# One change in five places of a two-layer diffusion kernel: half groups of first weights, other PSUM banks and earlier silus, split weights kept for a last pass run backwards

## The chip, the cores and the metric

One NeuronCore of one Trainium2 chip runs the whole program. The metric is the time of one execution in device microseconds (us). The core has five engines that work side by side and wait for each other by semaphores: TensorE (PE in the profile, and PEld for its weight loads), VectorE (DVE), ScalarE (ACT), GpSimd (POOL) and SyncE (SP, which only issues DMAs here). Each engine takes its instructions strictly in the order in which the program was built.

## The reference

Two post-norm layers over 256 latent tokens and 256 context tokens of width 2048, in float32.

```python
for l in range(DEPTH):                       # DEPTH = 2
    shift_l, scale_l, gate_l = split(silu(c) @ mod_w[l] + mod_b[l], 3)      # the same from c_ctx for the context
    hl = xl * (1.0 + scale_l) + shift_l;  hc = xc * (1.0 + scale_c) + shift_c
    if l % 2 == 0:   # one input projection, 2048 -> 6400: pooling mixer | RWKV-7 in both directions
        yl, yc = (concat([multiscale_pool(a), rwkv], -1) * silu(gate)) @ w_out
    else:            # one input projection: attention of 16 heads with 4 key heads, rotary, RMSNorm of q and k
        yl = (attention(q, k, v) * silu(g)) @ w_out
    xl = layer_norm(ALPHA * xl + gate_l * yl)   # and xc likewise after layer 0; the output is xl
```

## The kernel before

Each large product is made three times from split operands: a weight or an activation is cast to fp32r by ScalarE (`whi`, `hh`), the rest `x - hi` is taken by VectorE or GpSimd (`wlo`, `hl`), and `mm3` runs hi·hi, hi·lo and lo·hi, each a matmul of 512 columns ("wide" below), into one PSUM bank. All weights come from HBM for each use. There are eight banks under the tags `acc`, `tr` and `prep` (two each), `cx` and `cz` (one each).

The order of TensorE's instructions is fixed by hand when the program is built: the parts of the kernel are generators that a small loop (`merge`) steps in turn by priority and by a reckoned clock `self.t`; a `yield` of a number says after how many reckoned us a generator wants to go on, a `yield` of a process that it waits for that process's end. The orders of the other engines are set by the tile framework, which places instructions by a timeline of its own, and earlier if they are marked `high_priority`. The helper `run_fill` takes a list of units (a source in HBM and a function that makes the matmuls), loads `rawbufs - 1` units ahead and splits one unit ahead.

The stages, in order:

- `begin`. Eight groups `g`. The modulation weights (`modA`, eight loads of 512 KB for a group: four for the shift, four for the scale) meet the conditioning vector in narrow matmuls (`prep<-wrow,sc`); the row that results is copied, turned into columns (`prep<-comb,wrow`) and applied to two 128-row tiles of x (`modulate`, which appends the split tiles to `self.h`). Then the first six chunks of the input projection use these two tiles, three chunks for each of two `wF` loads (384 KB): `first(g, 0)` and `first(g, 1)`, 18 wide matmuls each. The units stand in the order: the eight modulation units of group g+1, then `first(g, 0)`, `first(g, 1)`. The buffers for raw weights are eight of 1024 columns.
- The middle. `rwkv` with its helpers (`lora` first) is a long chain of small matmuls; `fill0`, at a lower priority, fills TensorE with the other 44 chunks of the input projection, and `gemvs` computes the modulation of layer 1 and the gates from `modB`. Each chunk ends in `spill`, which for the 16 gate chunks applies `silu` (L315 to L319: two ScalarE steps, a VectorE step between them, a third ScalarE step, and a VectorE product that reads the bank for the last time).
- `out0`, the output projection of layer 0 in passes of 512 output columns: pass 0 over the banks acc, acc, tr, tr, pass 1 over prep, prep, cx, cz, pass 2 over the first set again, then columns 3 in two halves. Its activations `y[k]` are made by `gated_acts` and `gate_acts`: 16 products, each cast by ScalarE (L78, `hh`) and subtracted by VectorE or GpSimd (L74, `hl`) in turn. Their pool takes the place of the pool of `self.h`, so they start when the last input chunk is done.
- `norm0`, twice: LayerNorm of two token tiles, transposes to `prep`, then the modulation of layer 1 as (x·A + B) from PSUM on VectorE (`hraw`, L989), a cast and a subtraction. GpSimd meanwhile applies the LayerNorm's weights to the other copy (L1004, L1005: 32 steps).
- `layer1`: keys, values, queries, gates, attention heads, filled like the middle.
- `out1`, the output projection of layer 1: passes over columns 0, 1, 2 for both token tiles, then columns 3 for tile 0 and for tile 1, each with all 16 weights loaded and split anew. `final(t)` normalises: two steps each on ScalarE and VectorE, the weight `lg` on VectorE, the bias `lb` on VectorE or GpSimd, and four stores.

## Time and profile before

| what | value |
|---|---|
| time, median of 3 runs | 1881.06 us (1879.25 to 1887.59) |
| the profiled execution: its time, its span | 1879.39 us, 1877.6 us |
| TensorE busy | 1711.6 us, 91% of the span |
| VectorE, ScalarE, GpSimd busy | 1048.8, 728.6, 660.8 us |
| granted clock, mean over the span | 0.964 |

Time minus span is 1.8 us, which the trace doesn't show. TensorE is the engine with the least idle time; "PEclk" is the share of full speed that its clock was granted, where 1.00 is 2.4 GHz and 0.50 is 1.2 GHz.

### The profile page before, as it was taken

What the parts mean: (1) busy time and instruction counts of PE and PEld (TensorE: products, weight loads), DVE (VectorE), ACT (ScalarE), POOL (GpSimd) and SP (SyncE); (2) the same over time, 40 slices, a digit from 0 to 9 for tenths busy, and PEclk for the clock granted to TensorE, in tenths of its full rate; (3) what the DMA queues carried; (4) which work ended last, traced back from release to release, by engine and by line L of the source; (5) the groups of instructions that cost most, each with busy time, mean ns of one, the idle gap of its engine ahead of it and who ended that gap; (6) DMA issues with size and microseconds to landing.
All of it is one profiled execution on the core that took longest, in us unless ns stands there. A gap on an engine that the chain in (4) does not pass through costs nothing. (4 is left out here: it accounts for less than half of the span.)

```text
span 1877.6 us, 38910 instructions
## 1 busy us (share of the span) xinstructions
PE 1711.6 (91%) x15584; PEld 1286.9 (69%) x15584; DVE 1048.8 (56%) x1992; ACT 728.6 (39%) x1402; POOL 660.8 (35%) x565
## 2 busy tenths in 40 slices
PE   6888989999999999999997899699988999999995
PEld 3656666666676666677675577588766878888773
DVE  2224467666676758384845522411495487666458
ACT  1115634242425242434332243322453455555444
POOL 1114233323232324142413344544655442231234
PEclk9889999999999989899989999899999999999998
DMA  9886844544544445454456454444653543443754
GB/s 377 298 316 198 301 157 152 164 148 147 157 155 157 164 129 166 126 175 157 138 164 197 145 183 138 127 127 129 205 152 128 160 150 112 127 135 96 258 192 166
DMA packets 162213, 322.72 MB, mean 172 GB/s; under 512 B 17648, under 2 KB 28400, under 8 KB 160880
## 3 DMA queue, kind: packets, MB, share of 16 engines
q1 hardware_dynamic: 153680, 299.15, 49.0%
q10 hardware_dynamic: 8352, 21.09, 3.5%
q8 instruction: 122, 2.00, 0.4%
q14 instruction: 59, 0.48, 0.1%
HBM read 290.25 MB, written 29.92 MB: 171 GB/s over the span
## 5 line engine op out<-in xcount | busy, mean ns | idle before, releaser
L74 POOL TENSOR_TENSOR wlo<-wrow,whi 128x512 fp32r<-128x512 f32 (+1 forms) x347 | 474.6, 1370 | 948.8 <-ACT whi L206 842.6
L206 ACT CAST whi<-wrow 128x512 fp32r<-128x512 f32 (+1 forms) x528 | 328.3, 625 | 609.3 <-PE acc L87 189.2
L87 PE MATMUL acc<-hh,whi 128*128 128x512 f32 (+1 forms) x992 | 385.9, 389 | 11.7 <-ACT whi L206 9.0
L87 PE MATMUL acc<-hh,wlo 128*128 128x512 f32 (+1 forms) x992 | 384.8, 388 | 7.3 <-POOL wlo L74 3.6
L87 PE MATMUL acc<-hl,whi 128*128 128x512 f32 (+1 forms) x992 | 383.4, 387 | 0.0
L87 PEld LDWEIGHTS acc<-hh,whi 128*128 128x128 f32 x992 | 190.5, 192 | 56.1 <-ACT whi L206 13.0
L87 PEld LDWEIGHTS acc<-hh,wlo 128*128 128x128 f32 x992 | 190.7, 192 | 51.8 <-issue 9.0
L87 PEld LDWEIGHTS acc<-hl,whi 128*128 128x128 f32 x992 | 190.5, 192 | 43.7 <-issue 12.4
L74 DVE TENSOR_TENSOR wlo<-wrow,whi 128x512 fp32r<-128x512 f32 (+1 forms) x181 | 144.1, 802 | 134.6 <-ACT whi L206 134.2
L87 PE MATMUL tr<-wlo,hh 128*128 128x512 f32 x224 | 91.0, 406 | 6.6 <-DVE wlo L74 3.4
L87 PE MATMUL tr<-whi,hl 128*128 128x512 f32 x224 | 90.5, 404 | 0.0
L87 PE MATMUL tr<-whi,hh 128*128 128x512 f32 x224 | 89.8, 401 | 0.0
L87 PE MATMUL prep<-gw,sc 128*32 128x128 f32 x2048 | 79.4, 287 | 8.8 <-issue 5.2
L87 PEld LDWEIGHTS prep<-gw,sc 128*32 128x32 f32 x2048 | 53.4, 113 | 17.6 <-issue 7.8
L87 PE MATMUL acc<-whi,hh 128*128 128x512 f32 x128 | 52.1, 407 | 13.4 <-DVE ev L319 11.8
L87 PEld LDWEIGHTS tr<-wlo,hh 128*128 128x128 f32 x224 | 42.5, 190 | 18.3 <-DVE wlo L74 5.1
L87 PE MATMUL acc<-wlo,hh 128*128 128x512 f32 x128 | 52.1, 407 | 3.0 <-POOL wlo L74 3.0
L87 PE MATMUL prep<-wrow,sc 128*32 128x256 f32 x512 | 39.0, 444 | 17.3 <-DMA wrow<-in_modA 17.2
L461 POOL TENSOR_TENSOR BK<-T,D 64x512 f32<-64x512 f32 x32 | 46.4, 1451 | 23.2 <-PE cz L87 11.8
L87 PE MATMUL acc<-whi,hl 128*128 128x512 f32 x128 | 51.9, 406 | 0.5 <-DVE hl L74 0.5
L87 PEld LDWEIGHTS tr<-whi,hh 128*128 128x128 f32 x224 | 42.5, 190 | 10.6 <-issue 0.5
L87 PEld LDWEIGHTS tr<-whi,hl 128*128 128x128 f32 x224 | 42.5, 190 | 9.9 <-issue 0.7
(373 smaller groups left out, 3096.4 us busy)
## 6 DMA issues: line engine op xcount, KB each, us to landing
gw<-in_modB SPq DMA_DIRECT2D x256, 256.0 KB
wrow<-in_wA SPq DMA_DIRECT2D x176, 256.0 KB
wrow<-in_modA SPq DMA_DIRECT2D x64, 512.0 KB
wrow<-in_w SPq DMA_DIRECT2D x112, 256.0 KB
wrow<-in_woA SPq DMA_DIRECT2D x80, 256.0 KB
wrow<-in_wo SPq DMA_DIRECT2D x80, 256.0 KB
wrow<-in_w1g SPq DMA_DIRECT2D x64, 256.0 KB
pd<-ev SPq DMA_DIRECT2D x50, 256.0 KB
```

What stands on the lines that cost most here:

```text
L74: e.tensor_tensor(out=out, in0=raw, in1=hi.bitcast(F32), op=ALU.subtract)
L87: self.nc.tensor.matmul(out, a, b, start=start, stop=stop)
L206: self.lastsplit = self.nc.scalar.copy(hi, raw)
L461: nc.gpsimd.tensor_tensor(out=BK[hs, :, 1 - h, :], in0=c8(k)[hs], in1=c8(ew)[hs], op=ALU.mult)
```

## The change

Five places change together.

1. `begin`: the units stand in half groups: four modulation units of group g+1, `first(g, 0)`, the other four, `first(g, 1)`. Since `first(g, 0)` now comes nearer to the modulation that it needs, it waits (in the planning) until `self.h` holds its tiles. `gemvs` plans its first step 20 us after the start of the middle instead of 10.
2. `spill`: the gates' silus are marked `high_priority`. `out0`: the two sets of banks are swapped, so that pass 0 uses prep, prep, cx and cz and waits, in the planning, for the end of `rwkv` and `gemvs`, which used these banks. The banks of keys and values in `layer1` are swapped to match.
3. `norm0`: every second pair of tiles gets its A and B on ScalarE instead of VectorE, and the planned step between pairs is 1.6 us instead of 1.0.
4. `out1`: in the fourth pass (columns 3, tile 0) the last six split weights are kept; the fifth (tile 1) runs over the 16 weights backwards and takes those six without loading or splitting them. From the third pass on there are 7 buffers for raw and 9 for split weights (before: 8 and 5).
5. `final`: z·lg is computed ahead on GpSimd, slice by slice; then three of four slices take two VectorE steps (b = lg·r1 + lb, z = z·r0 + b), and the first takes two ScalarE and two GpSimd steps.

```diff
--- before.py
+++ after.py
@@ -182,14 +182,17 @@
 
     def run_fill(self, units):
 
         units = list(units)
         raws, splits = [], []
         for i, (_, f, *_) in enumerate(units):
             while len(raws) < min(len(units), i + self.rawbufs - 1):
-                raws.append(self.load(units[len(raws)][0]))
+                src = units[len(raws)][0]
+                raws.append(src if isinstance(src, int) else self.load(src))
             while len(splits) < min(len(units), i + 2):
-                splits.append(raws[len(splits)] if len(units[len(splits)]) > 2 else self.split(raws[len(splits)]))
-            yield from f(splits[i])
+                raw = raws[len(splits)]
+                splits.append(raw if isinstance(raw, int) or len(units[len(splits)]) > 2 else self.split(raw))
+            yield from f(self.kept[splits[i]] if isinstance(splits[i], int) else splits[i])
             raws[i] = splits[i] = None
 
     def row(self):
@@ -278,6 +281,8 @@
 
             def first(g, half):
                 def f(w):
+                    while len(self.h) < 2 * g + 2:
+                        yield 0.3
                     for i in range(3):
                         for j in range(2):
                             k = 2 * g + j
@@ -288,9 +293,8 @@
             mods = [self.mod_cols(0, 2 * g, 256, "prep") + self.mod_cols(1, 2 * g, 256, "prep", lambda g=g: modulate(g)) for g in range(8)]
             units = list(mods[0])
             for g in range(8):
-                if g < 7:
-                    units += mods[g + 1]
-                units += [first(g, 0), first(g, 1)]
+                m = mods[g + 1] if g < 7 else []
+                units += m[:4] + [first(g, 0)] + m[4:] + [first(g, 1)]
             self.merge(self.spawn(self.run_fill(units), 9))
             self.wset(wp, 512, 4, 3)
         for m, a in zip(self.FIRST, acc):
@@ -301,7 +305,8 @@
         if m < M_G:
             self.nc.scalar.copy(ev, ps)
         else:
-            self.silu(ev, ps)
+            with self.tc.high_priority():
+                self.silu(ev, ps)
         self.nc.sync.dma_start(self.pd[m], ev)
         self.there.add(m)
 
@@ -808,7 +813,7 @@
         biases(0)
         for _ in range(3):
             ahead()
-        yield 10.0
+        yield 20.0
         bank, ends = self.pt("prep"), []
         for r in range(256):
             i, k = divmod(r, KT)
@@ -846,14 +851,17 @@
 
     GPACE = 7.0
 
-    def outproj(self, w, y, ks, passes, done):
-        acc = {}
+    def outproj(self, w, y, ks, passes, done, keep=0):
+        acc, self.kept = {}, {}
 
         def unit(j, i, k):
             n, toks, tags = passes[j]
 
             def g(wt):
+                if keep and j == len(passes) - 2 and i >= KT - keep:
+                    self.kept[k] = wt
                 if i == 0:
                     acc[j] = [self.pt(t, bufs=1 if t in ("cx", "cz") else None) for t in tags]
                 if j == 0 and callable(y[k]):
@@ -862,9 +870,12 @@
                     yield from self.mm3(a, wt, y[k], i == 0, i == KT - 1, slice(0, 512), slice(t * 128, t * 128 + 128), flip=True)
                 if i == KT - 1:
                     yield from done(n, toks, acc.pop(j))
+            if keep and j == len(passes) - 1 and i < keep:
+                return k, g
             return w[n, k // 2][:, k % 2 * 512:k % 2 * 512 + 512], g
 
-        return self.run_fill([unit(j, i, k) for j in range(len(passes)) for i, k in enumerate(ks)])
+        ks = list(ks)
+        return self.run_fill([unit(j, i, k) for j in range(len(passes)) for i, k in enumerate(ks[::-1] if keep and j == len(passes) - 1 else ks)])
 
     def gated_acts(self, main):
 
@@ -956,8 +967,10 @@
                 return self.y[k] or ys[k]
 
         yield self.joined
+        yield main
+        yield self.gemv_p
         self.norms, self.h1at = [], {}
-        a, b = ("acc", "acc", "tr", "tr"), ("prep", "prep", "cx", "cz")
+        b, a = ("acc", "acc", "tr", "tr"), ("prep", "prep", "cx", "cz")
         passes = [(0, range(4), a), (1, range(4), b), (2, range(4), a), (3, (0, 1), b[:2]), (3, (2, 3), b[2:])]
         yield from self.outproj(io["woA"], Y(), self.korder, passes, done)
 
@@ -986,13 +999,16 @@
                     self.tp(tp[:, k - k0, t * 128:t * 128 + 128], z[2 * s + t][:, k * 128:k * 128 + 128], self.cst["ident"])
             raw = lp.tile([128, 2, 256], F32, tag="hraw", name="hraw", bufs=2)
             for k in (k0, k0 + 1):
-                nc.vector.tensor_scalar(raw[:, k - k0, :], tp[:, k - k0, :], self.A[:, k, s:s + 1], self.B[:, k, s:s + 1], op0=ALU.mult, op1=ALU.add)
+                if k0 % 4:
+                    nc.scalar.activation(raw[:, k - k0, :], tp[:, k - k0, :], AF.Identity, scale=self.A[:, k, s:s + 1], bias=self.B[:, k, s:s + 1])
+                else:
+                    nc.vector.tensor_scalar(raw[:, k - k0, :], tp[:, k - k0, :], self.A[:, k, s:s + 1], self.B[:, k, s:s + 1], op0=ALU.mult, op1=ALU.add)
                 hh, hl = self.h1[k]
                 w = slice(s * 256, s * 256 + 256)
                 nc.scalar.copy(hh[:, w], raw[:, k - k0, :])
                 self.sub(hl[:, w], raw[:, k - k0, :], hh[:, w], "v")
                 self.h1at[s, k] = self.t + 3.0
-            yield 1.0
+            yield 1.6
         if s:
 
             lg = self.bcast(lp, io["lng"][0:1, :], "gb0")
@@ -1063,9 +1079,9 @@
         self.kpost = []
         lat, ctx4 = (2, 3), range(4)
 
-        units = self.proj(4, (0, 1), ("tr", "tr"), self.keys)
-        units += self.proj(5, ctx4, ("acc", "acc", "cx", "cz"), self.values)
-        units += self.proj(4, lat, ("tr", "tr"), self.keys)
+        units = self.proj(4, (0, 1), ("cx", "cz"), self.keys)
+        units += self.proj(5, ctx4, ("acc", "acc", "tr", "tr"), self.values)
+        units += self.proj(4, lat, ("cx", "cz"), self.keys)
         yield from self.run_fill(units)
         for p in self.norms:
             yield p
@@ -1251,21 +1267,33 @@
                 nc.vector.tensor_tensor(out=tmp, in0=a, in1=gb[:, w], op=ALU.mult)
                 nc.vector.scalar_tensor_tensor(out=z[t][:, w], in0=z[t][:, w], scalar=ALPHA, in1=tmp, op0=ALU.mult, op1=ALU.add)
                 self.bn(lp, z[t], t, n)
+                if n == 2:
+                    yield loads
+                    for i in range(3):
+                        v = slice(i * 512, i * 512 + 512)
+                        nc.gpsimd.tensor_tensor(out=z[t][:, v], in0=z[t][:, v], in1=lg[:, v], op=ALU.mult)
                 if n == 3:
-                    yield loads
+                    nc.gpsimd.tensor_tensor(out=z[t][:, w], in0=z[t][:, w], in1=lg[:, w], op=ALU.mult)
                     final(t)
             if n == 1:
                 self.l1p.__exit__(None, None, None)
-                self.wset(self.ctx.enter_context(self.tc.tile_pool(name="wlast", bufs=1)), 512, 8, 5)
+                self.wset(self.ctx.enter_context(self.tc.tile_pool(name="wlast", bufs=1)), 512, 7, 9)
             yield 0.0
 
         def final(t):
             rs = self.norm(lp, t)
             for n in range(4):
                 w = slice(n * 512, n * 512 + 512)
-                self.apply(rs, z[t][:, w], n % 2)
-                nc.vector.tensor_tensor(out=z[t][:, w], in0=z[t][:, w], in1=lg[:, w], op=ALU.mult)
-                (nc.vector if n % 2 else nc.gpsimd).tensor_tensor(out=z[t][:, w], in0=z[t][:, w], in1=lb[:, w], op=ALU.add)
+                b = lp.tile([128, 512], F32, tag="fb", name="fb", bufs=2)
+                if n:
+                    nc.vector.scalar_tensor_tensor(out=b, in0=lg[:, w], scalar=rs[:, 1:2], in1=lb[:, w], op0=ALU.mult, op1=ALU.add)
+                    nc.vector.scalar_tensor_tensor(out=z[t][:, w], in0=z[t][:, w], scalar=rs[:, 0:1], in1=b, op0=ALU.mult, op1=ALU.add)
+                else:
+                    nc.scalar.activation(b, lg[:, w], AF.Identity, scale=rs[:, 1:2])
+                    nc.scalar.activation(z[t][:, w], z[t][:, w], AF.Identity, scale=rs[:, 0:1])
+                    nc.gpsimd.tensor_tensor(out=b, in0=b, in1=lb[:, w], op=ALU.add)
+                    nc.gpsimd.tensor_tensor(out=z[t][:, w], in0=z[t][:, w], in1=b, op=ALU.add)
                 nc.sync.dma_start(io["out"][t * 128:(t + 1) * 128, w], z[t][:, w])
 
         class Y(list):
@@ -1273,7 +1301,7 @@
                 return self.y1[k] or (lambda: self.until(k))
 
         passes = [(0, (0, 1), ("acc", "acc")), (1, (0, 1), ("tr", "tr")), (2, (0, 1), ("acc", "acc")), (3, (0,), ("tr",)), (3, (1,), ("tr",))]
-        yield from self.outproj(io["wo1"], Y(), range(KT), passes, done)
+        yield from self.outproj(io["wo1"], Y(), range(KT), passes, done, 6)
 
     def until(self, k):
         while self.y1[k] is None:
```

The order of the loads that SyncE issues at the beginning, `modA` being modulation weights, `wA` weights of the middle that are loaded ahead, and `wF` the first chunks' weights. Before:

```order
L146 DMA par<-in_par 128x340
L200 DMA wrow<-in_modA 128x1024 x9
L200 DMA wrow<-in_wA 128x512 x4
L200 DMA wrow<-in_modA 128x1024 x6
L200 DMA wrow<-in_wA 128x512 x3
L200 DMA wrow<-in_modA 128x1024
L200 DMA wrow<-in_wF 128x768 x2
L200 DMA wrow<-in_modA 128x1024 x8
L200 DMA wrow<-in_wF 128x768 x2
```

Now:

```order
L146 DMA par<-in_par 128x340
L203 DMA wrow<-in_modA 128x1024 x9
L203 DMA wrow<-in_wA 128x512 x4
L203 DMA wrow<-in_modA 128x1024 x3
L203 DMA wrow<-in_wF 128x768
L203 DMA wrow<-in_modA 128x1024 x2
L203 DMA wrow<-in_wA 128x512 x3
L203 DMA wrow<-in_modA 128x1024 x2
L203 DMA wrow<-in_wF 128x768
L203 DMA wrow<-in_modA 128x1024 x4
L203 DMA wrow<-in_wF 128x768
```

The first `wF` now stands behind 12 loads of `modA` and 4 of `wA` instead of 16 and 7, and from there on one `wF` follows each four `modA`, where two followed each eight.

GpSimd's order where the input projection ends and pass 0 of `out0` begins (`hl` are the halves of y, `wlo` those of weights; the first row ends with the weights of units 0 and 1 of pass 0). Before:

```order
L74 TENSOR_TENSOR wlo<-wrow,whi 128x512 x36
L74 TENSOR_TENSOR hl<-AR_12222,hh 128x512
L74 TENSOR_TENSOR hl<-AR_12269,hh 128x512
L74 TENSOR_TENSOR hl<-GR_12330,hh 128x512
L74 TENSOR_TENSOR hl<-GR_12385,hh 128x512
L74 TENSOR_TENSOR hl<-AR_12432,hh 128x512
L74 TENSOR_TENSOR hl<-AR_12487,hh 128x512
L74 TENSOR_TENSOR hl<-GR_12574,hh 128x512
L74 TENSOR_TENSOR wlo<-wrow,whi 128x512
L74 TENSOR_TENSOR hl<-GR_12743,hh 128x512
L74 TENSOR_TENSOR wlo<-wrow,whi 128x512 x74
```

Now:

```order
L74 TENSOR_TENSOR wlo<-wrow,whi 128x512 x36
L74 TENSOR_TENSOR hl<-AR_12225,hh 128x512
L74 TENSOR_TENSOR hl<-AR_12286,hh 128x512
L74 TENSOR_TENSOR hl<-GR_12333,hh 128x512
L74 TENSOR_TENSOR hl<-GR_12388,hh 128x512
L74 TENSOR_TENSOR hl<-AR_12435,hh 128x512
L74 TENSOR_TENSOR hl<-AR_12490,hh 128x512
L74 TENSOR_TENSOR hl<-GR_12572,hh 128x512
L74 TENSOR_TENSOR wlo<-wrow,whi 128x512 x4
L74 TENSOR_TENSOR hl<-GR_12741,hh 128x512
L74 TENSOR_TENSOR wlo<-wrow,whi 128x512 x71
```

The weights of unit 2 still stand behind seven `hl`; what moved is that four weights instead of one come before the last `hl`. On ScalarE, too, the last gate's second and third silu step (L317 and L318, now L322 and L323) stay behind 14 casts of `hh`.

VectorE's order at the end (`z_18370` is token tile 0, `z_18371` tile 1; `tmp<-tr` is the first reading of the last pass's bank). Before:

```order
L778 TENSOR_SCALAR z_18370<-z_18370,rs 128x512 x2
L74 TENSOR_TENSOR wlo<-wrow,whi 128x512
L1267 TENSOR_TENSOR z_18370<-z_18370,lg 128x512 x4
L1268 TENSOR_TENSOR z_18370<-z_18370,lb 128x512
L1251 TENSOR_TENSOR tmp<-tr,gb 128x512
L1268 TENSOR_TENSOR z_18370<-z_18370,lb 128x512
L1252 SCALAR_TENSOR_TENSOR z_18371<-z_18371,tmp 128x512
L763 BN_STATS bns<-z_18371 128x6
```

Now:

```order
L1290 SCALAR_TENSOR_TENSOR fb<-lg,rs,lb 128x512
L1291 SCALAR_TENSOR_TENSOR z_18370<-z_18370,rs,fb 128x512
L1290 SCALAR_TENSOR_TENSOR fb<-lg,rs,lb 128x512
L1291 SCALAR_TENSOR_TENSOR z_18370<-z_18370,rs,fb 128x512
L1290 SCALAR_TENSOR_TENSOR fb<-lg,rs,lb 128x512
L1267 TENSOR_TENSOR tmp<-tr,gb 128x512
L1291 SCALAR_TENSOR_TENSOR z_18370<-z_18370,rs,fb 128x512
L1268 SCALAR_TENSOR_TENSOR z_18371<-z_18371,tmp 128x512
L768 BN_STATS bns<-z_18371 128x6
```

No weight is split any more among the last steps of tile 0, but one step of tile 0 still stands between the two readings for tile 1.

Of TensorE's order three counts matter. Between the input chunks' start and the first matmul of `lora` there were 65 wide matmuls and a step of `gemvs`, and now 70 and none. Between two groups of four transposes in the second `norm0` there were 5 wide matmuls, and now 7. On GpSimd's side of the same stretch, the 32 steps on z have 4 splits of weights among them before and 5 now.

## Rows read from the trace of the kernel before

**Rows 1.** The page: span, busy times, the group of weight splits on GpSimd.

```profile
span 1877.6 us, 38910 instructions
...
PE 1711.6 (91%) x15584; PEld 1286.9 (69%) x15584; DVE 1048.8 (56%) x1992; ACT 728.6 (39%) x1402; POOL 660.8 (35%) x565
...
L74 POOL TENSOR_TENSOR wlo<-wrow,whi 128x512 fp32r<-128x512 f32 (+1 forms) x347 | 474.6, 1370 | 948.8 <-ACT whi L206 842.6
```

**Rows 2.** Windows in `begin` (length; PE, PEld, DVE, ACT, POOL busy; clock, DMA, GB/s).

```profile
28.00:45.20 17.20, 13.43 (x69) 9.51 (x66) 7.51 (x16) 4.14 (x6) 2.55 (x2) 1.00 1.03 403
45.20:49.40 4.20, 4.20 (x53) 2.70 (x55) 0.27 (x1) 0.00 (x0) 0.00 (x0) 1.00 0.52 180
49.40:63.10 13.70, 11.52 (x61) 8.69 (x54) 4.58 (x11) 2.91 (x4) 1.81 (x1) 0.75 1.00 350
```

**Rows 3.** The same view, by stages of the program.

```profile
35.70:158.00 122.30, 109.80 (x729) 80.47 (x730) 36.72 (x74) 24.13 (x34) 15.55 (x10) 0.92 0.78 282
158.00:184.60 26.60, 20.28 (x94) 14.93 (x93) 14.24 (x12) 17.56 (x27) 16.66 (x18) 0.87 0.92 277
...
1393.80:1429.70 35.90, 26.71 (x119) 20.00 (x118) 35.33 (x54) 14.26 (x34) 35.39 (x39) 0.95 0.27 81
1829.50:1858.10 28.60, 24.85 (x97) 17.05 (x96) 28.12 (x40) 19.11 (x32) 14.21 (x9) 1.00 0.62 202
```

**Rows 4.** DMA issues: count and KB each.

```profile
wrow<-in_modA SPq DMA_DIRECT2D x64, 512.0 KB
...
wrow<-in_wF SPq DMA_DIRECT2D x16, 384.0 KB
xt<-in_xT ACTq DMA_DIRECT2D x16, 256.0 KB
```

**Rows 5.** TensorE's timeline in `begin` (start, us; idle before, releaser).

```profile
35.73 0.79 PE L87 MATMUL acc<-hh,whi 128*128 128x512 f32 x1 [0.77 <-ACT whi L206]
...
65.80 3.66 PE L87 MATMUL prep<-wrow,sc 128*32 128x256 f32 x64
...
77.57 0.40 PE L87 MATMUL tr<-hh,whi 128*128 128x512 f32 x1
...
80.37 0.39 PE L87 MATMUL cx<-hh,whi 128*128 128x512 f32 x1
```

**Rows 6.** Timeline where pass 0 of `out0` starts.

```profile
1173.98 2.17 ACT L78 CAST hh<-AR 128x512 fp32r<-128x512 f32 x4
...
1175.19 3.44 POOL L74 TENSOR_TENSOR hl<-AR,hh 128x512 fp32r<-128x512 f32 x2 [0.26 <-ACT hh L78]
...
1184.12 3.42 DVE L74 TENSOR_TENSOR hl<-GR,hh 128x512 fp32r<-128x512 f32 x2
1185.29 1.71 POOL L74 TENSOR_TENSOR hl<-GR,hh 128x512 fp32r<-128x512 f32 x1
1187.46 0.67 DVE L319 TENSOR_TENSOR ev<-ev,acc 128x512 f32<-128x512 f32 x1
...
1188.19 0.79 PE L87 MATMUL acc<-whi,hh 128*128 128x512 f32 x1 [11.83 <-DVE ev L319]
...
1193.17 1.57 POOL L74 TENSOR_TENSOR wlo<-wrow,whi 128x512 fp32r<-128x512 f32 x1 [6.18 <-ACT whi L206]
```

**Rows 7.** Timeline in the second `norm0`.

```profile
1406.20 0.98 DVE L989 TENSOR_SCALAR hraw<-prep,mA,mB 128x256 f32<-128x256 f32 x2
...
1407.33 0.63 PE L101 MATMUL prep<-cc,z 128*128 128x128 f32 x4 [1.63 <-DVE hraw L989]
...
1414.14 0.51 PE L87 MATMUL tr<-wlo,hh 128*128 128x512 f32 x1 [3.06 <-POOL wlo L74]
```

**Rows 8.** Timeline of the end.

```profile
1857.67 0.40 PE L87 MATMUL tr<-whi,y1l 128*128 128x512 f32 x1
...
1863.67 0.69 DVE L763 BATCH_NORM_STATS2 bns<-z 128x6 f32<-128x512 f32 x1
...
1868.60 4.67 POOL L1268 TENSOR_TENSOR z<-z,lb 128x512 f32<-128x512 f32 x2 [5.51 <-DVE z L1267]
```

## The prediction

> **What bounds the kernel now.** I read the page first: TensorE is busy for 1711.6 of 1877.6 us, and no other engine comes near [rows 1]. The time can fall only where TensorE stands idle (166 us in all) or where its clock is below full; work on other engines counts only as a wait of TensorE. So I took TensorE's idle times in order of time, put windows around the stretches that the change touches, and read the timeline there. Five places matter.
>
> `begin` from the first wide matmul on (35.7) to its last spill (158.0): 122.3 us with TensorE busy for 109.8, so 12.5 idle; at a granted clock of 0.92 another 122.3 x 0.08 = 9.8 us go to slow cycles [rows 3]. The reason is in the finer windows: while TensorE runs at the DMAs' pace, these move 403 GB/s; then come some 4 us in which nothing frees a buffer and they fall to 180; then TensorE waits at a clock of 0.75 until the loads are back, at 350 [rows 2]. This repeats about six times.
>
> The stage of `lora` (158.0 to 184.6): 20.28 of 26.6 us busy [rows 3]. Pass 0 of `out0`: one wait of 11.83 us for the last silu step [rows 6]. The second `norm0`: 9.2 of 35.9 us idle, while VectorE (35.33) and GpSimd (35.39) are full [rows 3]. The last two passes (28.6 us, 24.85 busy, VectorE full at 28.12 [rows 3]) and the tail: the last matmul ends at 1858.07, 19.5 us before the span does [rows 8].
>
> The sum is made against the profiled execution, 1879.39 us (1.8 more than its span). It lies 0.09% below the median, so no correction is needed. About 0.5%, 9.4 us, is what a measurement of this kernel can tell from no change: faster means below about 1871.7.
>
> **The change part by part.**
>
> *Half groups.* A wide matmul takes (80.37 - 77.57) / 12 = 0.233 us, and a group's 64 narrow ones 3.66 [rows 5]. The first `wF` now stands behind four loads of `modA` and three of `wA` fewer. By the sizes [rows 4], and with `wA` at half a `modA`'s size, that is 4 x 0.524 + 3 x 0.262 = 2.88 MB, at 403 GB/s 7.1 us: the first wide matmul comes at 28.6. A half group is then 18 x 0.233 + 1.83 + about 0.36 for its columns = 6.4 us of TensorE against 2.75 MB of loads (four `modA`, one `wF`, one `xT`), 6.8 us at 403 GB/s or 7.9 at 350 [rows 2]. So the two run side by side with neither far ahead, where before a whole group was first all loads and then all matmuls. TensorE's work from the first wide matmul is 122.3 - 22.3 = 100 us at full clock, and 102 now, since 1.83 us of narrow matmuls move behind it. With no overhead the stage ends at 28.6 + 102.2 = 130.8 (27 gained); with all of the old overhead at 153.1 (5 gained). All loads of the beginning (64, 16 and 16 of those in [rows 4], seven `wA`, about 46.6 MB) take 115 us at 403 GB/s and 133 at 350, and some 15 us of work follow the last one. I take half the overhead, 11 us: it ends at 142. **Gain 16 (5 to 27).**
>
> *`lora`.* With `gemvs` moved back, five wide matmuls take the place of a step, but TensorE then waits for `lora`'s inputs, a chain of ScalarE and VectorE steps that doesn't get shorter; 6.3 us are idle [rows 3]. **Gain 1.5 (0 to 6.3).**
>
> *Pass 0.* The wait for the bank is gone, since `cx`, `cz` and `prep` have long been free there; the planned waits on `rwkv` and `gemvs` cost nothing, since both end well before the input projection does. The earlier silu changes nothing: its steps keep their place behind the casts on ScalarE. What is late next is `wlo` of unit 2. It still stands behind seven `hl` on GpSimd, the first from 1175.19, the last until 1187.0, at 1.7 us each [rows 6]; with a split of 1.37 [rows 1] it is there at 1188.3, when the old wait ended. In between TensorE can do units 0 and 1, 24 wide matmuls and one more, where it did 3: 22 x 0.233 = 5.1 us less 0.2. The bounds are nothing, and the whole wait with about 12 matmuls at half clock behind it (the first took 0.79 us [rows 6]), 11.8 + 12 x 0.233 = 14.6. **Gain 5 (0 to 14.6).**
>
> *`norm0`.* VectorE loses half of its `hraw` steps (0.49 us each [rows 7]), and seven wide matmuls instead of five, 1.6 us, stand between transposes: about the wait of 1.63 for `hraw`. But the longest wait, 3.06, is for GpSimd's `wlo` [rows 7], and GpSimd has five instead of four of those among its 32 steps on z. **Gain 4 (0 to 9.2).**
>
> *Last two passes.* 96 wide matmuls take 22.4 us if nothing holds them; the stretch has 28.6. Only the last pass loses splits, six, of which VectorE had most. **Gain 3 (0 to 6).**
>
> *Tail.* The bank is read and z finished before `bn` at 1863.67, 5.6 us after the last matmul [rows 8], since VectorE first does four products and biases of tile 0. Now one step of tile 0 stands between: some 3.0 us. From there GpSimd had two adds in 4.67 us [rows 8], and still has two. **Gain 3 (1 to 7).** Its eight z·lg steps stand among the splits of the passes before: 8 x 1.3 us of an engine with room, on an engine whose lateness TensorE sometimes sees. **Cost 1 (0 to 4).**
>
> One row speaks against that move. Beside a GpSimd subtraction VectorE's took 3.42 / 2 = 1.71 us, while its product after GpSimd was done took 0.67 [rows 6]. The Trainium skill, "SBUF — State Buffer", section "Who interferes with whom", says that a two-input VectorE operation on SBUF and a GpSimd one share a port pair which one holds for its whole instruction, while the other stands. The row agrees. By that rule each z·lg costs a VectorE step up to 1.3 us, and the cost above would be its upper bound.
>
> *The middle.* The same matmuls are planned anew; +-5.
>
> Sum: 16 + 1.5 + 5 + 4 + 3 + 3 - 1 = 31.5; 1879.4 - 31.5 = **1848**.
>
> **The rivals.**
>
> (a) Everything in `begin` is covered and the wait at pass 0 goes wholly: 27 + 14.6 + 1.5 + 4 + 3 + 3 - 1 = 52, so 1827. For it: TensorE and loads are near balance. Against it: `wlo` behind the `hl`. Chance 0.1.
>
> (b) The loads run at 350 GB/s, as in the stretches in which TensorE waits [rows 2]: 7.9 us for a half group of 6.4, so `begin` gains 5, and the places where VectorE or GpSimd is full give nothing: 5 + 5 + 3 + 2 - 1 = 14, so 1865. The Trainium skill, "DMA: Bandwidth & Descriptors", section "Where 436 GB/s comes from", has loads from HBM bound at about 358 GB/s; by that the loads take 130 us, an estimate, and the time comes out here. The 403 GB/s over 17 us [rows 2] disagree, the later 350 doesn't. Chance 0.15.
>
> (c) Gains and a worse plan of the middle meet within 0.5%: 1871 to 1889, 0.05.
>
> (d) Slower: with short waits in every half group, TensorE's clock falls to 1.2 GHz in them. The window at 0.75 [rows 2] shows that a wait is enough for that. A half group's 6.4 us become 12.8 at half clock. Five of the 16 eat the whole gain of all parts, seven end at 1848 + 7 x 6.4 = 1893, slower by 0.7%. Against it: 0.92 over the stage with waits of 2 to 4 us [rows 3], and these get shorter. Chance 0.03.
>
> That the silu part doesn't do what it says is in the sum already.
>
> **How the numbers follow.** My forecast has 0.67; (a) 0.1, (b) 0.15, (c) 0.05, (d) 0.03. The main case alone spans 1835 to 1860, from the bounds of `begin` and of pass 0, which hardly meet all at once. To leave out no more than 2 in 10 the range takes in (b) and the near part of (a): 1832 to 1866. Faster by over 0.5%: 0.67 + 0.1 + 0.15 = 0.92; within 0.5%: 0.05; slower: 0.03.
>
> **What would show it.** `begin`'s last spill near 142 instead of 158, with a first wide matmul near 28.6 and a DMA rate without the falls to 180; at 153 (b) holds. At pass 0 a wait of about 7 us ended by GpSimd's `wlo`; none, and (a) holds; 11 us, and the banks weren't it. In `norm0` GpSimd full as before. In the tail `bn` about 3 us after the last matmul and the end about 17 us after it. Wrong would be a clock below 0.85 in `begin` (d), a later end of the middle by more than 5 us, or VectorE steps of 1.7 us beside z·lg that make TensorE wait in passes 1 to 3.

## The result and the profile after

The changed kernel took 1857.91 us in the median of 4 runs (1853.62 to 1863.75) beside 1880.15 for the kernel before (4 runs): a ratio of 0.9897, 95% interval 0.9868 to 0.9926, or 22 us less. The forecast was 1848 within 1832 to 1866. Executions of one kernel spread by 10 to 26 us, so a part of a few us is read from its own stage and not from the whole time. The profiled execution took 1855.6 us, 23.8 less than that of before. The first two lines of its page answer to [rows 1]:

```profile
span 1853.8 us, 38879 instructions
...
PE 1697.3 (92%) x15584; PEld 1275.7 (69%) x15584; DVE 1038.0 (56%) x1968; ACT 729.1 (39%) x1412; POOL 675.2 (36%) x571
```

TensorE has 14.3 us less of busy time for the same 15584 matmuls, and the span is 23.8 us shorter: only some ten of these 24 are waits. So the comparison has to go stage by stage. Of before, the windows that were not shown yet (a group of `begin` at full clock; the middle, from the first `AR,U` matmul behind `lora` to the end of `rwkv`; `out0` to the first transpose of `norm0`; `norm0` and `layer1`; `out1`; the tail):

```profile
83.30:97.90 14.60, 13.42 (x113) 9.47 (x112) 5.63 (x11) 2.91 (x4) 1.30 (x1) 1.00 0.91 326
182.50:1078.40 895.90, 828.21 (x11097) 596.56 (x11096) 562.31 (x1098) 335.32 (x657) 293.70 (x279) 0.96 0.51 164
1174.60:1363.30 188.70, 174.38 (x725) 138.04 (x726) 61.48 (x87) 56.47 (x97) 102.85 (x76) 0.95 0.50 146
1363.30:1755.10 391.80, 370.94 (x2005) 304.61 (x2004) 270.47 (x564) 199.77 (x425) 138.80 (x113) 1.00 0.42 132
1755.10:1858.10 103.00, 95.16 (x394) 72.15 (x392) 61.71 (x88) 51.22 (x86) 37.02 (x26) 1.00 0.70 240
1858.10:1877.60 19.50, 0.00 (x0) 0.00 (x0) 12.04 (x23) 1.93 (x4) 9.18 (x4) 0.53 0.30 108
```

After, `begin` from its first wide matmul, one group of it, and then the same five stages (columns as in [rows 2]):

```profile
29.90:149.00 119.10, 108.73 (x761) 73.67 (x762) 35.65 (x75) 24.44 (x35) 17.84 (x11) 0.99 0.85 310
91.60:107.50 15.90, 14.05 (x113) 9.25 (x116) 4.99 (x11) 2.88 (x5) 2.88 (x2) 1.00 0.99 366
175.20:1066.40 891.20, 822.41 (x11116) 592.74 (x11118) 553.46 (x1097) 332.56 (x654) 296.80 (x278) 0.97 0.52 165
1162.80:1343.40 180.60, 174.30 (x725) 137.98 (x726) 56.33 (x87) 56.30 (x97) 103.48 (x76) 0.98 0.51 153
1343.40:1734.50 391.10, 371.38 (x2005) 306.43 (x2004) 266.87 (x548) 205.83 (x441) 138.17 (x113) 0.99 0.43 132
1734.50:1833.70 99.20, 93.19 (x394) 72.74 (x392) 65.41 (x81) 45.83 (x79) 47.01 (x31) 1.00 0.70 233
1833.70:1853.80 20.10, 0.00 (x0) 0.00 (x0) 15.32 (x22) 2.52 (x6) 7.40 (x5) 0.61 0.28 104
```

In that group the narrow matmuls come in two halves like this one, where [rows 5] has them in one piece of 3.66 us:

```profile
99.41 1.93 PE L87 MATMUL prep<-wrow,sc 128*32 128x256 f32 x32
```

The ends of the stages tell where the 23.8 us came from. `begin` ends at 149.03 instead of 157.97: 8.9 us, of which 5.8 are the earlier first wide matmul (29.93 instead of 35.73). The middle begins 7.3 us earlier, since the stretch between them takes 1.6 more, and ends 12.0 earlier. In it TensorE's idle time is 68.8 us where it was 67.7; its busy time is 5.8 less at a clock of 0.97 instead of 0.96, and that is more than the 4.7 us gained in a stage whose work was only planned anew. `out0` is 8.1 us shorter, `norm0` with `layer1` 0.7, `out1` 3.8, and the tail 0.6 longer.

Pass 0 of `out0`, from the timeline (start, length; idle before and releaser), answers to [rows 6]:

```profile
1172.05 0.40 PE L87 MATMUL prep<-whi,hh 128*128 128x512 f32 x1
...
1173.53 1.71 POOL L74 TENSOR_TENSOR hl<-GR,hh 128x512 fp32r<-128x512 f32 x1
1175.20 4.19 POOL L74 TENSOR_TENSOR wlo<-wrow,whi 128x512 fp32r<-128x512 f32 x3
...
1176.96 0.79 PE L87 MATMUL prep<-wlo,hh 128*128 128x512 f32 x1 [4.52 <-POOL wlo L74]
```

The wait of 11.83 us for the bank is now one of 4.52 for `wlo`, behind the seventh of GpSimd's eight `hl`. Since the first matmul of the pass, at 1162.75, 37 wide matmuls went ahead of it, so three units had their weights, and the one waited for is the fourth's: the first row of GpSimd's order, said to end with the weights of units 0 and 1, ends with those of unit 2. In the second `norm0` the four waits for `hraw`, 3.9 us together, are gone, and those for `wlo` there have grown from 6.1 to 9.5 us in all (5.3 to 7.0 for GpSimd's, 0.8 to 2.5 for VectorE's). The two longest:

```profile
1383.87 0.53 PE L87 MATMUL cx<-wlo,hh 128*128 128x512 f32 x1 [2.76 <-POOL wlo L74]
...
1391.48 0.79 PE L87 MATMUL cx<-wlo,hh 128*128 128x512 f32 x1 [2.52 <-POOL wlo L74]
```

In the tail VectorE comes to tile 0's steps (`fb`, L1290) as the last matmul ends, and to the last bank (`tmp`, L1267) 5.3 us after its end. `bn` starts 7.3 us after the last matmul, where [rows 8] have it after 5.6:

```profile
1833.26 0.39 PE L87 MATMUL tr<-whi,y1l 128*128 128x512 f32 x1
1833.34 0.75 DVE L1290 SCALAR_TENSOR_TENSOR fb<-lg,rs,lb 128x512 f32<-128x512 f32 x1
...
1834.56 1.52 POOL L1295 TENSOR_TENSOR fb<-fb,lb 128x512 f32<-128x512 f32 x1 [3.24 <-ACT fb L1293]
...
1834.99 1.63 DVE L1290 SCALAR_TENSOR_TENSOR fb<-lg,rs,lb 128x512 f32<-128x512 f32 x1
...
1838.99 0.68 DVE L1267 TENSOR_TENSOR tmp<-tr,gb 128x512 f32<-128x512 f32 x1
...
1840.97 0.69 DVE L768 BATCH_NORM_STATS2 bns<-z 128x6 f32<-128x512 f32 x1
```

### The profile page after: what moved, and what is told of

Same layout as the page of the kernel before. It is cut to its first block, busy times and chain, and to the rows that moved or that the text cites. A ratio compares the mean times of both kernels' runs of the same rounds, so it can differ in the third digit from the quotient of the medians.

```text
span 1853.8 us, 38879 instructions
## 1 busy us (share of the span) xinstructions
PE 1697.3 (92%) x15584; PEld 1275.7 (69%) x15584; DVE 1038.0 (56%) x1968; ACT 729.1 (39%) x1412; POOL 675.2 (36%) x571
## 5 line engine op out<-in xcount | busy, mean ns | idle before, releaser
L209 ACT CAST whi<-wrow 128x512 fp32r<-128x512 f32 (+1 forms) x522 | 323.9, 625 | 583.8 <-PE acc L87 188.4
L87 PE MATMUL acc<-hh,whi 128*128 128x512 f32 (+1 forms) x992 | 380.9, 384 | 5.9 <-ACT whi L209 3.5
L87 PE MATMUL acc<-hh,wlo 128*128 128x512 f32 (+1 forms) x992 | 378.7, 382 | 7.1 <-POOL wlo L74 3.6
L87 PEld LDWEIGHTS acc<-hh,whi 128*128 128x128 f32 x992 | 188.6, 190 | 49.4 <-issue 9.4
L87 PE MATMUL tr<-wlo,hh 128*128 128x512 f32 x192 | 77.7, 405 | 1.7 <-DVE wlo L74 0.9
L87 PE MATMUL tr<-whi,hl 128*128 128x512 f32 x192 | 77.3, 403 | 0.0
L87 PE MATMUL tr<-whi,hh 128*128 128x512 f32 x192 | 76.7, 399 | 0.4 <-ACT whi L209 0.4
L87 PE MATMUL tr<-AR,BK 64*128 64x128 f32 x512 | 43.1, 298 | 9.8 <-DVE GR L503 8.2
L87 PE MATMUL prep<-wrow,sc 128*32 128x256 f32 x512 | 38.1, 429 | 13.3 <-DMA wrow<-in_modA 13.3
L87 PEld LDWEIGHTS tr<-AR,BK 64*128 64x128 f32 x512 | 35.5, 197 | 19.3 <-issue 14.9
L654 DVE TENSOR_TENSOR R<-cz,NV 128x128 f32<-128x128 f32 x32 | 9.3, 290 | 62.8 <-PE cz L87 62.8
```

The lines of the kernel that those rows point to most:

```text
L87: self.nc.tensor.matmul(out, a, b, start=start, stop=stop)
L209: self.lastsplit = self.nc.scalar.copy(hi, raw)
L654: nc.vector.tensor_tensor(out=R, in0=cx, in1=NV[:, :, c, :], op=ALU.add)
```

## The experiments

A run's ratio is against the kernel before on the same chip.

**Parts alone.** Each is the kernel before with the lines of one or two points of the change. Only `p_banks` has an interval below 1; for the other three the time alone shows no gain, and the windows have to be read. The four ratios multiply to 0.991, about that of the whole change. `p_begin` (point 1):

```diff
-                units += [first(g, 0), first(g, 1)]
+                units += m[:4] + [first(g, 0)] + m[4:] + [first(g, 1)]
...
-        yield 10.0
+        yield 20.0
```

> The kernel before with point 1 of the change alone (half groups, gemvs planned from 20 us). The traces of before and after have the last spill of begin 8.9 us earlier, the first matmuls of lora as much, and the end of rwkv 12. If the point stands by itself, this run has the first wide matmul at 29.9, the end of begin at 149.0 and a time of 1880 - 9 to 12 = 1868 to 1871. If the gain needs the other points, or if a planned-anew middle made half of it, the time is 1874 or more with begin still ending at 149. By the term of the prediction (16) it would be 1864.

Measured: 1879.38 us (10 runs, 1860.25 to 1886.28) beside 1877.48; ratio 0.9982 (0.9950 to 1.0015). The windows of `begin` and of the middle:

```profile
30.00:147.70 117.70, 108.74 (x761) 74.24 (x762) 35.56 (x75) 24.39 (x35) 17.79 (x11) 0.99 0.86 313
173.70:1075.70 902.00, 834.38 (x11118) 601.09 (x11118) 556.70 (x1097) 332.86 (x654) 295.45 (x278) 0.95 0.51 163
```

`begin` ends at 147.7, 10.3 us earlier than before, with 9.0 us of idle time: the point does what it did in the whole change. But the middle takes 902.0 us. Its idle time is 67.6 us, as before; its busy time is 6 us longer at a clock of 0.95. What `begin` gave, this execution lost as slow clock. That its runs spread over 26 us says that others didn't: its fastest is 13 us below the fastest of 31 runs of before.

`p_banks` (banks and planned waits of point 2, no earlier silus):

```diff
-        a, b = ("acc", "acc", "tr", "tr"), ("prep", "prep", "cx", "cz")
+        b, a = ("acc", "acc", "tr", "tr"), ("prep", "prep", "cx", "cz")
...
```

> The kernel before with the swapped banks and the planned waits of point 2 alone, without the earlier silus. Theory: the banks are the whole of what was gained at pass 0; the wait of 11.83 us becomes one of about 4.5 ended by GpSimd's wlo, with some 36 wide matmuls done ahead of it, and the time is 1880 - 8 = 1872. Rival: the silus marked high_priority carry part of it, and the wait stays at 7 us or more, time 1875.

Measured: 1872.25 us (10 runs); ratio 0.9971 (0.9949 to 0.9994). `out0` to the first transpose, and the first and the waiting matmul of pass 0:

```profile
1167.80:1347.30 179.50, 174.79 (x726) 138.39 (x727) 59.61 (x87) 56.47 (x97) 103.21 (x76) 0.98 0.52 154
```

```profile
1167.84 0.50 PE L87 MATMUL prep<-whi,hh 128*128 128x512 f32 x1 [1.52 <-ACT hh L78]
...
1182.07 0.50 PE L87 MATMUL prep<-wlo,hh 128*128 128x512 f32 x1 [3.02 <-POOL wlo L74]
```

`out0` is 9.2 us shorter without the silus, and the wait is 3.0 us. The banks and the planned waits are the whole of this gain.

`p_norm0` (point 3; `nc.scalar.activation` for every second pair, `yield 1.6`):

```diff
+                if k0 % 4:
+                    nc.scalar.activation(raw[:, k - k0, :], tp[:, k - k0, :], AF.Identity, scale=self.A[:, k, s:s + 1], bias=self.B[:, k, s:s + 1])
...
-            yield 1.0
+            yield 1.6
```

> The kernel before with point 3 alone. Theory: GpSimd is full in the second norm0, so that the waits for hraw go and those for wlo grow by as much: the stretch from its first transpose to the first matmul of out1 is within 1 us of before, time 1879 to 1880. Rival, the prediction's term: 4 us less, 1876.

Measured: 1875.36 us (10 runs); ratio 0.9980 (0.9953 to 1.0007). `norm0` and `layer1`:

```profile
1355.50:1744.90 389.40, 370.50 (x2005) 305.85 (x2004) 265.99 (x548) 205.83 (x441) 138.16 (x113) 0.99 0.43 133
```

389.4 us instead of 391.8: 2.4 us, between the two expectations (within 1, and 4).

`p_last` (points 4 and 5):

```diff
-        yield from self.outproj(io["wo1"], Y(), range(KT), passes, done)
+        yield from self.outproj(io["wo1"], Y(), range(KT), passes, done, 6)
...
-                nc.vector.tensor_tensor(out=z[t][:, w], in0=z[t][:, w], in1=lg[:, w], op=ALU.mult)
+                    nc.vector.scalar_tensor_tensor(out=b, in0=lg[:, w], scalar=rs[:, 1:2], in1=lb[:, w], op0=ALU.mult, op1=ALU.add)
```

> The kernel before with points 4 and 5 alone. Theory: the passes of out1 are 3.8 us shorter and the tail 0.6 longer, because VectorE comes to tile 0's two steps for each slice only as the last matmul ends and does five of them ahead of the last bank: time 1877, tail 20 us. Rival, the prediction's terms: passes 3 shorter, tail 3 shorter, z on GpSimd costs 1: 1875, tail 16.5.

Measured: 1875.42 us (10 runs); ratio 0.9981 (0.9958 to 1.0003). Its middle, `out1` and the tail:

```profile
183.00:1067.70 884.70, 814.71 (x11095) 587.07 (x11095) 563.71 (x1098) 334.67 (x657) 293.48 (x279) 0.98 0.52 165
1745.00:1844.10 99.10, 92.84 (x394) 72.85 (x392) 64.16 (x81) 45.99 (x79) 46.75 (x31) 1.00 0.69 234
1844.10:1864.30 20.20, 0.00 (x0) 0.00 (x0) 15.38 (x22) 2.56 (x6) 7.41 (x5) 0.63 0.28 104
```

`out1` takes 99.1 us. Kernels without these points took 103.0 (before), 105.6 (`p_begin`), 105.3 (`p_norm0`), 105.2 (`p_banks`), 106.9 (`p_gemv20`), so the gain is 4 to 8. The tail is 20.2, as expected. The middle of this execution, whose TensorE order is that of before, took 884.7 us where before took 895.9.

**What bounds `begin`: `x_half`.** The changed kernel with half of each modulation weight loaded and read twice:

```diff
-        return [(w[:, q * 4 * n:(q + 1) * 4 * n], f(q), True) for q in range(4)]
+        return [(w[:, q * 4 * n:q * 4 * n + 2 * n], f(q), True) for q in range(4)]
...
```

> The changed kernel with half of each modulation weight left out: each of the 64 loads brings 512 instead of 1024 columns, and the narrow matmuls read these twice, so that TensorE's work is the same and 16.8 of the 46.6 MB of the beginning are not loaded. The modulation is then another one. Theory (the loads set the length of begin: from 45 to 105 us the DMAs are 98 to 100% busy at 361 to 369 GB/s): begin ends 10 us or more earlier than 149.0, at about 133, since 16.8 MB are 46 us of loading and TensorE's own 107 us become the bound, and TensorE's idle time between the first wide matmul and the end falls from 10.3 to 4 us or less. Rival (the splits' and the clock's own pace, not the loads): the first wide matmul comes 8 us earlier, but from there to the end it is 119 us as before with 10 us of idle time.

The loads of the changed kernel in four windows of `begin`, and then `x_half` from its first wide matmul to the end of `begin`:

```profile
45.00:60.00 15.00, 14.92 (x136) 9.89 (x128) 6.37 (x12) 3.11 (x5) 3.37 (x2) 1.00 1.00 369
60.00:75.00 15.00, 12.65 (x81) 8.91 (x81) 2.19 (x6) 1.67 (x2) 1.81 (x1) 0.89 0.89 311
75.00:90.00 15.00, 13.64 (x108) 8.86 (x107) 5.02 (x12) 2.90 (x4) 1.28 (x1) 1.00 1.00 361
90.00:105.00 15.00, 13.15 (x104) 8.44 (x103) 4.49 (x9) 2.90 (x4) 3.10 (x2) 1.00 0.98 365
```

```profile
24.30:137.10 112.80, 108.52 (x761) 76.23 (x762) 36.79 (x75) 24.51 (x35) 17.55 (x11) 0.94 0.62 203
```

In three of these windows the DMAs are busy for 98 to 100% and move 361 to 369 GB/s; the expectation's "from 45 to 105 us" leaves out the second, where they are at 0.89 and 311. With fewer loads `begin` ends 11.9 us earlier, at 137.1 (one run, 1839.92 us): 5.6 us are the earlier first wide matmul, and the idle time behind it falls from 10.4 to 4.3 us. The loads do hold it up. But TensorE's busy time stays at 108.5 (at a clock of 0.94): behind the loads stands TensorE's own work, hardly shorter than the stage.

**Pass 0: `x_hl_dve`.**

```diff
-            y = self.split_act(self.prod[k], 512, "vp"[n % 2])
+            y = self.split_act(self.prod[k], 512, "v")
```

> The changed kernel with all sixteen subtractions hl of pass 0's activations on VectorE instead of VectorE and GpSimd in turn. Theory: VectorE and GpSimd hold each other up (1.7 us for each hl on both, where a VectorE step alone takes 0.67), so VectorE does all of them in as long as it now does half; GpSimd is free for wlo, the wait of 4.52 us for wlo at pass 0 goes, the 7 us at half clock with it, and out0 to the first transpose is 6 to 8 us shorter than 180.7. Rival: VectorE takes 1.2 us for each, is then the late one (14 x 1.2 = 17 us instead of 12), and TensorE waits for hl as long or longer: 180.7 or up to 5 more.

Measured: 1846.71 us (4 runs, 1843.61 to 1855.87); ratio 0.9836 (0.9791 to 0.9882). `out0`, and VectorE's first four `hl` and GpSimd's `wlo` in pass 0:

```profile
1165.00:1341.10 176.10, 173.17 (x726) 137.17 (x727) 57.15 (x95) 56.27 (x97) 90.94 (x68) 0.99 0.52 156
```

```profile
1165.46 2.49 DVE L74 TENSOR_TENSOR hl<-AR,hh 128x512 fp32r<-128x512 f32 x4
...
1173.32 4.91 POOL L74 TENSOR_TENSOR wlo<-wrow,whi 128x512 fp32r<-128x512 f32 x3 [8.06 <-ACT whi L209]
```

Alone VectorE takes 2.49 / 4 = 0.62 us for an `hl`. `wlo` starts at once behind its cast, the wait is gone, and `out0` is 4.5 us shorter than 180.6; 6 to 8 were expected. Beside the other kept traces with the new banks, 178.5 to 180.7 us, it is 2.4 to 4.6. Of the kernels that leave nothing out it has, with `x_gemv10` below, the lowest ratio to before, but its interval meets that of the changed kernel (0.9868 to 0.9926), so that by time alone it isn't shown to be faster than that one; the two edits together were not tried.

**The tail: `x_tail`.** Tile 0's `fb` steps on VectorE get a dependency on tile 1's `bn`, and stand behind tile 1's norm in the program:

```diff
-                    nc.vector.scalar_tensor_tensor(out=b, in0=lg[:, w], scalar=rs[:, 1:2], in1=lb[:, w], op0=ALU.mult, op1=ALU.add)
+                    self.behind(nc.vector.scalar_tensor_tensor(out=b, in0=lg[:, w], scalar=rs[:, 1:2], in1=lb[:, w], op0=ALU.mult, op1=ALU.add), last)
...
```

> The changed kernel with VectorE's six steps of tile 0's final (slices 1 to 3) put behind the reading of the last bank, tile 1's z and its bn. Theory (order): the tail lost because five steps of tile 0 stand ahead of the last bank; bn comes at 1.5 us after the last matmul instead of 7.3, and the tail is 15 us instead of 20.1. Rival (one port for two engines): the two-input steps of VectorE and GpSimd take about 17 us together in any order, so bn is earlier but the end is within 2 us of 20.1.

Measured: 1856.39 us; ratio 0.9886 (0.9846 to 0.9927). Its middle and tail, and the timeline of the end:

```profile
173.90:1076.60 902.70, 833.92 (x11118) 601.10 (x11118) 554.29 (x1097) 332.92 (x654) 297.50 (x278) 0.95 0.51 163
1843.70:1863.20 19.50, 0.00 (x0) 0.00 (x0) 14.96 (x22) 2.55 (x6) 7.02 (x5) 0.62 0.29 108
```

```profile
1843.26 0.39 PE L87 MATMUL tr<-whi,y1l 128*128 128x512 f32 x1
...
1845.14 0.69 DVE L768 BATCH_NORM_STATS2 bns<-z 128x6 f32<-128x512 f32 x1
...
1847.61 1.18 DVE L748 TENSOR_TENSOR nwt<-nwt,mv 128x1 f32<-128x1 f32 x1
...
1852.02 1.59 POOL L1302 TENSOR_TENSOR z<-z,fb 128x512 f32<-128x512 f32 x1
1852.52 1.63 DVE L1297 SCALAR_TENSOR_TENSOR z<-z,rs,fb 128x512 f32<-128x512 f32 x1
```

`bn` comes 1.5 us after the last matmul, and the tail still takes 19.5 us. The theory that this order would gain falls. VectorE's steps take 0.7 us alone and 1.63 beside GpSimd's 1.59; from the last matmul on there are fourteen of them on 512 columns with two inputs, five such on GpSimd, and the norm's chain. An order makes these no fewer, but it can overlap them better: here VectorE had only the norm's narrow steps for 3.4 us between `bn` and the next `fb` (1845.87 to 1849.29; 2.1 in the changed kernel), two of them stretched to 0.76 and 1.18 us beside GpSimd. Tile 0's steps put into that stretch, or GpSimd's steps moved off it, were not tried.

**GpSimd in `norm0`: `x_nobias`.** The line with `in1=lb[:, w]` on GpSimd left out of `norm0`.

> The changed kernel with GpSimd's 16 additions of the LayerNorm's bias in the second norm0 left out (the residual of layer 1 then lacks it). Theory: GpSimd was full there and its wlo late, so with 16 of 32 steps gone the two waits of 2.8 and 2.5 us for wlo fall to under 1 each, and norm0 and layer 1 together (391.0 us) are 5 us shorter. Rival: the pace is set by VectorE and the transposes, and the stretch stays within 1.5 us.

```profile
1340.40:1722.20 381.80, 368.55 (x2004) 304.04 (x2003) 260.42 (x548) 205.28 (x441) 125.66 (x97) 1.00 0.44 136
```

381.8 instead of 391.1 us: 9.3 less, with 13.3 us of idle time instead of 19.7 (one run, 1843.07 us). The waits of 2.76 and 2.52 us are gone. GpSimd's steps were what this stretch waited for, more than was expected. How they held it up isn't told apart: VectorE's 548 steps, too, took 260.42 us instead of 266.87, and the wait for its `wlo` is shorter as well (0.78 us at most instead of 1.71).

**Later `gemvs`: `x_gemv10` and `p_gemv20`.** The changed kernel with `yield 10.0` again, and the kernel before with `yield 20.0` and nothing else.

> The changed kernel with gemvs' first step planned 10 us after the start of the middle again. So far five profiles of the new middle (later gemvs) took 890.6 to 902.7 us with 52 to 87 us at half clock, four of the old one 884.7 to 895.8 with 41 to 68, all with 68 to 70 us of idle time. Theory (the new plan of the middle costs): without the later step the middle is back at about 889, and the time is 5 us or more below that of the changed kernel on the same chip. Rival (the half clock falls by chance, whatever the plan): the two agree within 3 us.

> The kernel before with nothing but gemvs' first step at 20 instead of 10 us. Theory (the later step costs): the middle grows by some 6 us and the time is 3 to 7 us above before. Rival (chance): no difference beyond 3 us; the prediction's term for this step was a gain of 1.5.

> The changed kernel unchanged, for more executions on the same chip as the other three. Both theories: 21 us below before, the middle anywhere between 888 and 903 us by how long its clock is at half, and 68 to 70 us of idle time in it.

Measured on one chip, before at 1882.34 us (17 runs): `x_gemv10` 1852.17 (6 runs, 1843.52 to 1860.64; ratio 0.9825, 0.9792 to 0.9859), the changed kernel 1858.74 (6 runs, 1845.90 to 1863.77; ratio 0.9863, 0.9827 to 0.9898), `p_gemv20` 1884.92 (12 runs; ratio 1.0026, 1.0001 to 1.0052). Both medians say that the later step costs, some 3 and 7 us, but the intervals of `x_gemv10` and the changed kernel meet, and that of `p_gemv20` only just leaves out 1. The kept traces lean the same way: from the first `BK,U` matmul to the end of `rwkv` it is 882.7 to 899.6 us in the five with the earlier step (mean 889.6) and 890.2 to 902.3 in the nine with the later one (mean 895.2). The ranges overlap. The middle of `x_gemv10` was a long one:

```profile
171.80:1074.10 902.30, 836.80 (x11095) 600.17 (x11096) 561.77 (x1099) 337.04 (x658) 294.42 (x279) 0.95 0.51 163
```

65.5 us of idle time, the least of all, but a clock of 0.95 and 902.3 us. That the later step costs is likely and not shown; how it would, stays open. The second trace of the changed kernel (`after_again`) ends `begin` at 151.7 instead of 149.0, with 10.0 us of idle time and a clock of 0.96, and its middle takes 899.6 us.

**Later `wA`: `c_hl_wA`.** `x_hl_dve` with the loads planned from group 6 on, the seven `wA` among them, placed behind a split of that group:

```diff
-        self.nc.sync.dma_start(raw, src)
+        self.behind(self.nc.sync.dma_start(raw, src), self.hold)
...
```

> The changed kernel with all hl of pass 0 on VectorE, and with the seven wA loads of the beginning moved from before the first half group to the last three. Theory (loads set the length of begin): the first wide matmul comes 4 to 5 us earlier, at 25.3, since 1.8 MB fewer stand before it, and begin ends 4 us earlier, at 145; with out0 at 176 the time is 8 us below that of the changed kernel on the same chip. Rival (TensorE's 107 us of own work are as near a bound): the start is earlier, but the idle time in begin grows by as much, and only the 4.6 us of pass 0 are gained.

Measured: 1853.07 us (6 runs); ratio 0.9847 (0.9813 to 0.9880). `begin`, then GpSimd, VectorE and TensorE in its last group, and VectorE's same steps in `x_hl_dve`:

```profile
27.20:152.50 125.30, 112.93 (x761) 77.76 (x762) 39.13 (x75) 26.25 (x38) 22.04 (x14) 0.95 0.86 302
```

```profile
132.23 8.37 POOL L74 TENSOR_TENSOR wlo<-wrow,whi 128x512 fp32r<-128x512 f32 x5 [8.41 <-ACT whi L211]
...
135.94 4.80 DVE L280 TENSOR_SCALAR xt<-xt,modc 128x256 f32<-128x256 f32 x4
...
141.40 0.80 PE L87 MATMUL acc<-hl,whi 128*128 128x512 f32 x1 [2.54 <-DVE hl L74]
```

```profile
137.84 2.05 DVE L278 TENSOR_SCALAR xt<-xt,modc 128x256 f32<-128x256 f32 x4
```

The first wide matmul comes 2.7 us earlier, and `begin` ends 3.5 us later, with 12.4 us of idle time (one wait of 2.54 in the last group) and a clock of 0.95. The theory fails, and the rival holds: what was gained at the start is lost in `begin`. The long wait isn't for a load: it is for VectorE's `hl`, behind four `xt` steps that took 4.80 us beside GpSimd's splits of five `wA`, and 2.05 in `x_hl_dve`. How much of the 3.5 us is this wait and how much the clock, no run tells apart: `after_again`, without the edit, ended `begin` only 0.8 us earlier.

## Why the prediction was right, point by point

The time lies in the range and the sign was sure, but the sum of 31.5 was 8 to 10 too much; the first term alone missed by 7. That the total came as near as it did is in part luck: the terms that were too high (`begin`, `lora`, `norm0`, the tail) are partly made up by pass 0, which was too low, and by the middle of the one profiled execution. One pair of traces says little about a part of a few us. All kept traces, sorted by whether they hold the point (means in us, with the range; left out are runs that edit the stage otherwise, and for `norm0` the two that edit pass 0 ahead of it, with 387.6 and 387.7), give:

| stage | without | with | gain | forecast |
|---|---|---|---|---|
| end of `begin` | 158.9 (157.7 to 160.7) | 148.8 (147.7 to 151.7) | 10.1 | 16 |
| `begin`'s end to `BK,U` | 26.7 (26.6 to 26.9) | 26.6 (26.4 to 26.8) | 0.1 | 1.5 |
| the middle from `BK,U` | 889.6 (882.7 to 899.6) | 895.2 (890.2 to 902.3) | -5.6 | 0 |
| `out0` | 189.0 (188.6 to 189.5) | 179.5 (178.5 to 180.7) | 9.5 | 5 |
| `norm0` and `layer1` | 392.2 (391.7 to 393.3) | 390.4 (389.4 to 391.1) | 1.7 | 4 |
| `out1` | 105.2 (103.0 to 106.9) | 98.6 (97.4 to 99.7) | 6.6 | 3 - 1 |
| tail | 19.5 | 20.1 to 20.2 | -0.6 | 3 |

The gains add up to 21.8, and the medians differ by 22.2. The bullets give the profiled pair.

- **Half groups, 16 forecast, 8.9 measured.** The mechanism is right in kind: the loads fall less often (in windows of 3 us before the last loads, three times to between 194 and 251 GB/s, where they fell four times to between 97 and 251), and most of the slow clock is gone (0.99 instead of 0.92; 0.95 to 0.99 over the seven traces, 0.89 to 0.92 over the five without). The idle time and the little slow clock left are the half of the old overhead that was taken. The prediction's "about six times" read too much into its rows: the clock fell to half in four of the groups. Most of the 8.9, 5.8 us, is the earlier start. The size failed at "TensorE's work from the first wide matmul is 100 us at full clock, and 102 now". It is 107 to 108. A group of 113 instructions at full clock took 13.42 us busy before and 14.05 after: eight times 0.63 is 5.0 us, an estimate from one group, which smaller pieces cost and the sum didn't have. Of the 0.63 the narrow matmuls are 0.2 (twice 1.93 us instead of 3.66), the second change to them and back another 0.2 (the first wide matmul after it starts the next one after 0.34 us, not 0.23), and one more wait the rest. Another 1.3 us: the first wide matmul came at 29.9, not 28.6. With 102 the stage would have ended at the 142 that was forecast. Even with 36% of the bytes gone it ends only at 137.1.
- **`lora`, 1.5 forecast, nothing found.** From the end of `begin` to the first `BK,U` matmul it is 26.6 us before and 26.8 after, and 26.4 to 26.9 in all fourteen traces: the chain sets it, whatever TensorE does ahead of it. Over the whole run the later step seems to cost.
- **Pass 0, 5 forecast, 8.1 measured.** Right in all its steps but one: the wait went over to GpSimd's `wlo`, at 1176.96, which is about the 1188.3 of the forecast less the 11.9 us by which all had moved. But three units were split ahead, not two, so that 37 instead of 25 wide matmuls fill the wait. That the earlier silus add nothing to this is shown by `p_banks`.
- **`norm0`, 4 forecast, 0.7 measured (2.4 alone).** The step named GpSimd's `wlo` as the longest wait and still took half of the stalls as gained. What failed is that step: the 3.9 us of waits for `hraw` went, and most of them came back as waits for `wlo`. `x_nobias` shows that GpSimd's steps were the bound.
- **`out1`, 3 forecast, 3.8 measured (4 to 8 beside the other kernels).** Right, and rather too low; the cost of 1 for z·lg on GpSimd can't be read from the total. The slowed steps are there (z·lg takes 1.66 to 1.74 us beside VectorE in the passes, 1.26 alone in the tail), and two waits for weights next to them, of 0.35 and 0.74 us, would make up that 1.
- **Tail, 3 gained forecast, 0.6 lost.** The order was read rightly, but "one step of tile 0 now stands between" left out when VectorE begins: at the last matmul's end, since the last pass's splits are ahead of tile 0's norm. Five steps of tile 0 then come first, some at 1.63 us. And `x_tail` shows that the place of `bn`, on which the term rested, doesn't set the end by itself. The Trainium skill, "SBUF — State Buffer", section "Who interferes with whom", has VectorE's two-input steps and GpSimd's stand for each other; the 1.63 us beside GpSimd and 0.75 without it, and 0.62 for an `hl` in `x_hl_dve`, agree.
- **The middle, nothing forecast within 5, 4.7 gained.** By the idle time nothing happened; the clock of that one execution did it. It is luck: over all kept traces the new plan's middle is the longer one.

Rival (b), loads at 350 GB/s, was half right: from 45 to 105 us they average 351, and 361 to 369 in the windows in which they are full, under the 403 of the sum; but `begin` gained more than its 5. The Trainium skill, "DMA: Bandwidth & Descriptors", section "Where 436 GB/s comes from", has 358; an average of 351 and windows at 361 to 369 lie near it, [rows 2] at 403 do not, and neither do single stretches of 3 us in the changed kernel, up to 422.

## What to carry to other kernels

Halving the pieces in which the loads and TensorE alternate brought the first piece forward and shortened the waits, but each switch cost TensorE something: look for a stretch at full clock and count busy time per instruction before summing. When a wait is removed, count how far every operand behind it is ready, unit by unit. And where an engine is full, as GpSimd in the second `norm0`, or busy for most of a stage and slowed by another, as VectorE in the tail (15.3 of 20.1 us), the reorderings tried here gave little; moving work off the full engine gave 2.4 to 4.6 us at pass 0 in one line.

## What the runs showed of the hardware

The same program's time spreads by 15 us (31 runs of before) to 26 us (10 runs of `p_begin`), and it goes with TensorE's mean granted clock (`p_begin`: 0.974 at 1860.25 us, 0.962 at 1886.28). In the six middles for which a window stands above, the idle time is 65.5 to 70.0 us, while the busy time for nearly the same matmuls (11,095 to 11,118) goes from 814.7 (clock 0.98, `p_last`) to 836.8 (0.95, `x_gemv10`), and the stage from 884.7 to 902.7 us (`x_tail`). `p_last` and before have the same order on TensorE there and differ by 11.2 us; after and `x_tail`, by 11.5. That is more than most of the parts tested here gain, which is why parts were judged by the windows of their own stage.
